# Ordering a three-block transformer kernel by a simulated timeline instead of the default heuristic

## The chip, the cores and the metric

The kernel runs on one core of a Trainium2 chip. A core has five engines with an instruction stream each: TensorE (PE in the profile, its weight loads PEld) multiplies matrices, VectorE (DVE), ScalarE (ACT) and GpSimd (POOL) work on tiles, and SyncE (SP) starts the DMA transfers. The engines meet only at semaphores. The metric is the device time of one execution in microseconds. Before the change it is 2908.86 us, the median of 3 runs from 2906.74 to 2912.71.

## The reference

The input is 512 tokens of 1024 numbers, which pass through three blocks in a row.

- The first block: RMS norm, one wide projection, sparse attention of 16 heads (compressed, selected and windowed keys, gated), a causal convolution of width 31 per channel with a layer norm behind it, an output projection, and a SwiGLU feed-forward layer.
- The second block: multi-scale pooling beside a gated delta net of 8 heads, an output projection with layer norm, an MLP with squared ReLU, and a gated side input. The delta net per head, cut to its core:

```
q, k, v = silu(conv4(x @ w))        # q and k normalised to length 1
m  = strictly_lower(beta * k @ k.T * decay)
u, w = solve(m + I, [v * beta, k * beta * exp(gc)])
for chunk n:                        # the recurrence
    v_new = u[n] - w[n] @ state
    o[n]  = qg[n] @ state + attn[n] @ v_new
    state = state * exp(gl[n]) + kg[n].T @ v_new
o = rms_norm(o) * o_norm_w * silu(z)
```

- The third block: stick-breaking attention (weights from a running sum of log-sigmoids along the keys) beside sliding-window attention, again with output projection, an MLP with squared ReLU, and a gated side input.

## The kernel before

All activations are kept transposed, as tiles of 128 features by 512 tokens. A gemm (`K.gemm`, L171 to L173) makes 128 output features: eight input tiles times three matmuls, since both weights and activations are split into a high and a low part (wh with the high part of the operand, wh with the low one, wl with the high one). Its result lies in a PSUM tile `pg`. A weight unit of 512 KB comes by DMA on SyncE into `wst` (2 buffers), ScalarE makes `wh` from it (L155), GpSimd `wl` (L156), with 4 buffers each. The gemms of the MLPs and projections make most of TensorE's work; the attention, the convolution and the delta net put small matmuls and much work of the other engines between them.

The delta net (`block2`) takes the heads one by one. `head_in` projects k, q and v of the next head (a gemm, a convolution of four taps L1308 to L1310, silu L1312 to L1313, normalisation L1321 to L1344). `chunks` builds the matrices of the head: transposes into KG and VB (L1371 to L1376), products of k with k and q (L1391) into MT and AT, the diagonal blocks written to memory and read back rearranged (dg, diag, B: DMA), their inverse Z by 30 small VectorE operations (L1416, L1417), Yi (L1420) and its transpose (L1425). Then come the levels 16, 32 and 64 of the inverse, each of which is a chain between TensorE and the others:

```
ps = MT.T @ Xi         # L1431   T1 = ps * level     # L1433 VectorE
ps = Yi.T @ T1         # L1437   Xi = Xi - ps        # L1439 VectorE
ps = transpose(Xi)     # L1443   Yi = copy(ps)       # L1445 ScalarE
last level: ps = T1.T @ Yi  # L1448   Yf = Yi - ps   # L1450 VectorE
```

`recur` runs the recurrence over four chunks of 128: k with the state S (L1462), t (L1464, VectorE), Yf with t (L1466), vn (L1468, ScalarE), the new state (L1471 on TensorE, S of L1474 or L1476 on VectorE), outputs into `po` (L1478, L1479), and then the output's copy, square, column sum (L1483, L1485, L1487) and norm (L1490). `merge` gates the output with two more gemms.

In the third block, `stick_scores` makes a head's scores (L1882 to L1884), takes them through exponent, logarithm, maximum, four scans and a last exponent into a weight tile z (L1887 to L1898), and `stick_mix` transposes z (L1907), splits it into PTh and PTl (L1779, L1780) and multiplies it with the values (L1909, L1910). `window_mix` (L1854 to L1858) does so for the windows.

In the first block VectorE has, beside the attention's operations, the 240 taps of the convolution (L673, on tiles `py`); ScalarE copies each finished channel tile (X, L674).

What sets the order: the kernel's text writes the work of the heads in an order given by strings of letters (`ORD`, `ORD2`, `ORD3`: which step of which generator comes next). The framework then orders the whole program anew. It plays the program on a model of the machine and takes, engine by engine, the ready instruction of the best priority; the priority goes by the text's position, shifted where the text says so: weight loads forward by `HP` (30, 60 and 0 places in the three blocks), the Z operations back by `SLO` = 50, the convolution's taps back by `LOW` = 3000. The order so made is fixed in the program; on the chip each engine runs its list from the front.

## Time and profile before

| what | value |
|---|---|
| median of 3 runs | 2908.86 us (2906.74 to 2912.71) |
| the profiled execution's own time | 2904.16 us |
| its span | 2902.4 us |
| mean granted TensorE clock | 0.972 |
| TensorE busy | 2676.3 us (92%) |
| VectorE busy | 1780.9 us (61%) |
| ScalarE busy | 1283.2 us (44%) |
| GpSimd busy | 1306.6 us (45%) |

Names of tiles stand in the profile without their numbers: `pg <- op,wh` is a matmul that reads the tiles op and wh and writes pg. L171 is line 171 of the kernel. "PE x <- DVE y" in a list of waits says that TensorE stood still ahead of the instruction that writes x until VectorE had written y. The granted clock is a share of the full clock. Idle time of an engine counts only where the chain that ends last passes over it.

### The profile page before, as it was taken

What the parts mean: (1) busy time and instruction counts of PE and PEld (TensorE: products, weight loads), DVE (VectorE), ACT (ScalarE), POOL (GpSimd) and SP (SyncE); (2) the same over time, 40 slices, a digit from 0 to 9 for tenths busy, and PEclk for the clock granted to TensorE, in tenths of its full rate; (3) what the DMA queues carried; (4) which work ended last, traced back from release to release, by engine and by line L of the source; (5) the groups of instructions that cost most, each with busy time, mean ns of one, the idle gap of its engine ahead of it and who ended that gap; (6) DMA issues with size and microseconds to landing.
All of it is one profiled execution on the core that took longest, in us unless ns stands there. A gap on an engine that the chain in (4) does not pass through costs nothing.

```text
span 2902.4 us, 34153 instructions
## 1 busy us (share of the span) xinstructions
PE 2676.3 (92%) x12206; PEld 2120.0 (73%) x12206; DVE 1780.9 (61%) x2825; ACT 1283.2 (44%) x2317; POOL 1306.6 (45%) x1023
## 2 busy tenths in 40 slices
PE   7899999699999988988889999999988889999997
PEld 5677776478888856766676788877766678788885
DVE  7889899965243596776774821126877765422246
ACT  4357875533222354444443533332556652322234
POOL 6554432554444454333332644454544344444443
PEclk9999999799999999999999999999999899999999
DMA  3321111232322222222222222232222122222223
GB/s 115 114 86 54 54 38 37 77 105 91 98 95 94 95 67 96 70 78 73 70 70 68 67 101 95 95 116 88 94 89 75 49 80 87 92 98 95 95 95 102
DMA packets 79193, 243.32 MB, mean 84 GB/s; under 512 B 11312, under 2 KB 15320, under 8 KB 79024
## 3 DMA queue, kind: packets, MB, share of 16 engines
q1 hardware_dynamic: 79024, 241.15, 25.3%
q8 instruction: 96, 1.57, 0.2%
q14 instruction: 73, 0.60, 0.1%
HBM read 230.96 MB, written 4.52 MB: 81 GB/s over the span
## 4 chain that ended last, share of the span: by engine, by line
PE 63%; DVE 23%; ACT 6%; DMA 3%; issue 3%; POOL 2%; SPq 0%; DVEq 0%; ACTq 0%; POOLq 0%
PE pg L172 18%; PE pg L173 18%; PE pg L171 18%; DMA B<-diag 2%; DVE p L1894 1%; DVE py L673 1%; DVE X L336 1%; DVE QK L1310 1%; PE ppt L956 1%; POOL wl L156 1%; DMA diag<-dg 1%; DVE ln L277 1%; DVE Zt L1416 1%; PE ps L934 1%; DVE Z L1417 1%
## 5 line engine op out<-in xcount | busy, mean ns | idle before, releaser
L156 POOL TENSOR_TENSOR wl<-wst,wh 128x512 fp32r<-128x512 f32 (+1 forms) x808 | 1099.9, 1367 | 1367.1 <-ACT wh L155 1285.7
L155 ACT ACTIVATE wh<-wst 128x512 fp32r<-128x512 f32 (+1 forms) x808 | 500.8, 627 | 1102.1 <-PE pg L172 918.1
L171 PE MATMUL pg<-op,wh 128*128 128x512 f32 (+1 forms) x2008 | 812.7, 405 | 38.9 <-ACT wh L155 19.5
L172 PE MATMUL pg<-op,wh 128*128 128x512 f32 (+1 forms) x2008 | 808.6, 403 | 2.6 <-DVE op L191 2.4
L173 PE MATMUL pg<-op,wl 128*128 128x512 f32 (+1 forms) x2008 | 807.2, 402 | 3.9 <-POOL wl L156 3.9
L171 PEld LDWEIGHTS pg<-op,wh 128*128 128x128 f32 (+1 forms) x2008 | 386.7, 193 | 120.9 <-ACT wh L155 20.1
L173 PEld LDWEIGHTS pg<-op,wl 128*128 128x128 f32 (+1 forms) x2008 | 386.2, 192 | 83.6 <-POOL wl L156 6.7
L172 PEld LDWEIGHTS pg<-op,wh 128*128 128x128 f32 (+1 forms) x2008 | 387.3, 193 | 82.2 <-DVE op L191 5.8
L171 PE MATMUL pg<-hid,wh 128*128 128x512 f32 x688 | 272.2, 396 | 0.9 <-DVE hid L190 0.9
L173 PE MATMUL pg<-hid,wl 128*128 128x512 f32 x688 | 272.1, 396 | 0.0
L172 PE MATMUL pg<-hid,wh 128*128 128x512 f32 x688 | 271.8, 395 | 0.2 <-DVE hid L191 0.2
L673 DVE SCALAR_TENSOR_TENSOR py<-z,vec,py 128x512 f32<-128x512 f32 x240 | 180.2, 751 | 10.9 <-ACT py L671 6.2
L1120 DVE TENSOR_TENSOR X<-X,pg 128x512 f32<-128x512 f32 x56 | 38.5, 688 | 222.1 <-PE pg L173 222.1
L171 PEld LDWEIGHTS pg<-hid,wh 128*128 128x128 f32 x688 | 129.2, 188 | 32.9 <-DVE hid L190 1.3
L172 PEld LDWEIGHTS pg<-hid,wh 128*128 128x128 f32 x688 | 129.2, 188 | 31.9 <-DVE hid L191 0.5
L173 PEld LDWEIGHTS pg<-hid,wl 128*128 128x128 f32 x688 | 129.2, 188 | 31.3 <-issue 0.2
L190 DVE CAST hid<-t 128x512 fp32r<-128x512 f32 x86 | 53.0, 616 | 145.7 <-ACT t L1097 145.0
L1111 DVE SCALAR_TENSOR_TENSOR t<-pg,R 128x512 f32<-128x512 f32 x32 | 22.1, 691 | 84.0 <-PE pg L173 83.9
L938 ACT ACTIVATE P<-ps,s 128x128 f32<-128x128 f32 (+3 forms) x128 | 66.4, 523 | 11.6 <-DVE s L937 9.5
L191 DVE TENSOR_TENSOR hid<-t,hid 128x512 fp32r<-128x512 f32 x86 | 63.6, 740 | 3.0
L937 DVE TENSOR_REDUCE s<-ps 128x1 f32<-128x128 f32 (+3 forms) x128 | 60.1, 483 | 8.1 <-PE ps L936 6.6
L960 DVE TENSOR_TENSOR PTl<-ppt,PTh 128x512 fp32r<-128x512 f32 x80 | 53.4, 684 | 4.7 <-ACT PTh L959 3.9
(523 smaller groups left out, 4344.3 us busy)
## 6 DMA issues: line engine op xcount, KB each, us to landing
wst<-in_w_f_dram SPq DMA_DIRECT2D x64, 512.0 KB
wst<-in_w_up_dram SPq DMA_DIRECT2D x32, 512.0 KB
wst<-in_w_down_dram SPq DMA_DIRECT2D x32, 512.0 KB
wst<-in_w_ga_dram SPq DMA_DIRECT2D x24, 512.0 KB
wst<-in_w_fg_dram SPq DMA_DIRECT2D x22, 512.0 KB
wst<-in_w_fu_dram SPq DMA_DIRECT2D x22, 512.0 KB
wst<-in_w_q_dram SPq DMA_DIRECT2D x16, 512.0 KB
wst<-in_w_out_dram SPq DMA_DIRECT2D x16, 512.0 KB
```

What stands on the lines that cost most here:

```text
L155: nc.scalar.activation(h, st, AF.Copy)
L156: nc.gpsimd.tensor_tensor(l, st, h, SUB)
L171: self.nc.tensor.matmul(ps, lhsT=wh, rhs=h[:, sl], start=first and k == 0, stop=False)
L172: self.nc.tensor.matmul(ps, lhsT=wh, rhs=l[:, sl], start=False, stop=False)
L173: self.nc.tensor.matmul(ps, lhsT=wl, rhs=h[:, sl], start=False, stop=last and k == n - 1)
L190: nc.vector.tensor_copy(h, src)
L191: nc.vector.tensor_tensor(l, src, h, SUB)
L673: nc.vector.scalar_tensor_tensor(y, z[:, k:k + T], w(k), y, op0=MUL, op1=ADD)
L937: nc.vector.tensor_reduce(mx[:, h:h + 1], S[:, :L], AX, MAX, negate=True)
L938: nc.scalar.activation(Pt[h][:, :L], S[:, :L], AF.Exp, bias=mx[:, h:h + 1], accum_out=den[:, h:h + 1])
L960: nc.vector.tensor_tensor(tl, pt, th, SUB)
L1120: nc.vector.tensor_tensor(X[:, m], X[:, m], ps, ADD)
```

## The change

One argument is added where the framework's context is opened. The framework then orders the whole program by a simulated timeline of all its engines instead of by its default heuristic. The text of the computation, the priorities and the number of buffers stay.

```
-    with tile.TileContext(nc) as tc:
+    with tile.TileContext(nc, schedule_with_timeline_sim=True) as tc:
         program(tc, I, out)
```

No matmul, activation, vector operation or DMA of the computation is added or removed. What differs is the order of each engine's list, and with it some semaphore instructions (on ScalarE 1048 for 997, on VectorE 254 for 225, on GpSimd 927 for 916) and table loads (74 for 77). The lists are the same, or nearly so, in the three MLPs; they differ in the first block's attention and convolution, in the delta net, and in the third block's attention.

The first place is TensorE in the middle of one delta-net head, at the second and third level of the inverse. `pg` rows are the gemm of another head's projection, `piv` are the inverse's tiles. Before:

```order
L1431 MATMUL piv_11054<-Xi_10975,MT_10781 128x128 x4
L172 MATMUL pg_11158<-op_9370,wh_11165 128x512
L173 MATMUL pg_11158<-op_9369,wl_11166 128x512
L171 MATMUL pg_11158<-op_9375,wh_11165 128x512
L172 MATMUL pg_11158<-op_9376,wh_11165 128x512
L1437 MATMUL piv_11061<-T_2380_11059,Yi_10982 128x128 x4
L173 MATMUL pg_11158<-op_9375,wl_11166 128x512
L171 MATMUL pg_11158<-op_9381,wh_11165 128x512
L172 MATMUL pg_11158<-op_9382,wh_11165 128x512
L173 MATMUL pg_11158<-op_9381,wl_11166 128x512
L1443 MATMUL piv_11068<-ident,Xi_11066 128x128 x4
```

and after the change, from the last gemm row ahead of the same steps:

```order
L173 MATMUL pg_11603<-op_9387,wl_11611 128x512
L1443 MATMUL piv_10977<-ident,Xi_10975 128x128 x4
L1431 MATMUL piv_11054<-Xi_10975,MT_10781 128x128 x4
L1437 MATMUL piv_11061<-T_2380_11059,Yi_10982 128x128 x4
L1443 MATMUL piv_11068<-ident,Xi_11066 128x128 x4
L1431 MATMUL piv_11143<-Xi_11066,MT_10781 128x128 x4
L1448 MATMUL piv_11150<-Yi_11073,T_2401_11148 128x128 x4
L1371 MATMUL piv_11204<-ident,QK_10811 128x128 x4
L1375 MATMUL piv_11210<-ident,vT_11008 128x128 x4
L1466 MATMUL prc_11247<-VB_10758,Yf_11155 128x128
L1391 MATMUL piv_11228<-QK_10811 128x256 x2
L1471 MATMUL prc_11251<-vn_11249,KG_10757 128x128
```

The gemm rows between the steps of the inverse are gone from there; they stand ahead of the first L1443 here, 41 gemm rows in a run with one step (L1437) among them. L1371, L1375 and L1391 belong to the next head, L1466 and L1471 are the first steps of this head's recurrence.

The second place is TensorE in the same head's recurrence, in its third chunk and after it. `prc` and `po` are the recurrence's tiles. Before:

```order
L1462 MATMUL prc_11429<-S_11321,QK_10366 128x128
L1478 MATMUL po_11246<-qg_10772,S_11321 128x128
L171 MATMUL pg_11454<-op_9327,wh_11457 128x512
L172 MATMUL pg_11454<-op_9328,wh_11457 128x512
L1466 MATMUL prc_11433<-t_2470_11431,Yf_11155 128x128
L173 MATMUL pg_11454<-op_9327,wl_11458 128x512
L171 MATMUL pg_11454<-op_9333,wh_11457 128x512
L1471 MATMUL prc_11437<-vn_11435,KG_10757 128x128
L1479 MATMUL po_11246<-AT_10782,vn_11435 128x128
L172 MATMUL pg_11454<-op_9334,wh_11457 128x512
L173 MATMUL pg_11454<-op_9333,wl_11458 128x512
L1462 MATMUL prc_11443<-S_11439,QK_10366 128x128
```

and after the change, from the third chunk's L1466 to the head's end:

```order
L1466 MATMUL prc_11433<-t_2470_11431,Yf_11155 128x128
L1471 MATMUL prc_11437<-vn_11435,KG_10757 128x128
L1479 MATMUL po_11246<-AT_10782,vn_11435 128x128
L1462 MATMUL prc_11443<-S_11439,QK_10366 128x128
L1478 MATMUL po_11246<-qg_10772,S_11439 128x128
L1466 MATMUL prc_11447<-t_2476_11445,Yf_11155 128x128
L1479 MATMUL po_11246<-AT_10782,vn_11449 128x128
L1487 MATMUL prc_11524<-os_11522,ones 128x512
L171 MATMUL pg_11815<-op_9327,wh_11818 128x512
```

Two gemm matmuls stood between L1462 and L1466, and between L1466 and L1471; now the third and fourth chunk follow each other without any, up to the output's column sum (L1487), behind which the next gemm starts.

The third place is TensorE at the end of the third block's attention, where the last head's weight tile z_19557 is transposed. `pg` rows are gemms of the output's gates. Before:

```order
L173 MATMUL pg_19770<-oo_17962,wl_19763 128x512
L171 MATMUL pg_19770<-oo_18279,wh_19762 128x512
L1907 MATMUL ppt_19633<-ident,z_19557 128x128 x4
L1907 MATMUL ppt_19644<-ident,z_19557 128x128 x3
L172 MATMUL pg_19770<-oo_18280,wh_19762 128x512
L173 MATMUL pg_19770<-oo_18279,wl_19763 128x512
L171 MATMUL pg_19770<-oo_18283,wh_19762 128x512
L1909 MATMUL po_19632<-PTh_19638,VA_19549 128x512
L172 MATMUL pg_19770<-oo_18284,wh_19762 128x512
L173 MATMUL pg_19770<-oo_18283,wl_19763 128x512
L1910 MATMUL po_19632<-PTl_19639,VA_19549 128x512
L1909 MATMUL po_19632<-PTh_19648,VA_19549 128x384
```

and after the change:

```order
L1910 MATMUL po_19590<-PTl_19607,VA_19549 128x384
L1907 MATMUL ppt_19621<-ident,z_19349 128x128
L1909 MATMUL po_19590<-PTh_19615,VA_19549 128x256
L1910 MATMUL po_19590<-PTl_19616,VA_19549 128x256
L1907 MATMUL ppt_19633<-ident,z_19557 128x128 x4
L1909 MATMUL po_19590<-PTh_19623,VA_19549 128x128
L1910 MATMUL po_19590<-PTl_19624,VA_19549 128x128
L1907 MATMUL ppt_19644<-ident,z_19557 128x128 x3
L1907 MATMUL ppt_19654<-ident,z_19557 128x128 x2
L1909 MATMUL po_19632<-PTh_19638,VA_19549 128x512
L1910 MATMUL po_19632<-PTl_19639,VA_19549 128x512
L1909 MATMUL po_19632<-PTh_19648,VA_19549 128x384
```

The gemm rows are gone from between the transposes (L1907) and the mix-in steps (L1909, L1910); ahead of these rows now stand the mix-in steps of the head before (po_19590), and no gemm since that head's scores.

## Rows read from the trace of the kernel before

**Rows 1.** The page: busy time by engine, and the chain that ended last.

```profile
PE 2676.3 (92%) x12206; PEld 2120.0 (73%) x12206; DVE 1780.9 (61%) x2825; ACT 1283.2 (44%) x2317; POOL 1306.6 (45%) x1023
...
PE 63%; DVE 23%; ACT 6%; DMA 3%; issue 3%; POOL 2%; SPq 0%; DVEq 0%; ACTq 0%; POOLq 0%
```

**Rows 2.** Stages: start:end, length, PE, PEld, DVE, ACT, POOL busy, PEclk, DMA share, GB/s.

```profile
500.00:550.00 50.00, 24.02 (x82) 16.89 (x81) 45.40 (x61) 19.40 (x28) 18.07 (x10) 0.69 0.06 21
...
1100.00:1600.00 500.00, 437.52 (x2126) 338.94 (x2126) 334.98 (x688) 225.86 (x368) 172.73 (x147) 0.96 0.24 75
...
1700.00:2050.00 350.00, 348.16 (x1510) 283.06 (x1509) 107.51 (x148) 116.29 (x196) 164.03 (x126) 1.00 0.29 98
2050.00:2400.00 350.00, 305.82 (x1391) 238.50 (x1390) 266.39 (x411) 201.53 (x358) 163.45 (x114) 0.94 0.24 77
```

**Rows 3.** TensorE's waits from 1150 to 1600: us in total, times, longest.

```profile
PE prc L1462 <- DVE S L1474: 18.2, 5, 5.3
PE prc L1466 <- DVE t L1464: 7.7, 5, 3.6
PE piv L1425 <- DVE Yi L1420: 7.0, 6, 2.3
PE piv L1391 <- DVE KG L1372: 5.1, 5, 1.2
```

**Rows 4.** The chain, 1350 to 1445: start, length, what.

```profile
1352.98 1.13 PE piv L1391 x4
...
1357.05 4.43 DMA diag<-dg
...
1361.54 7.05 DMA B<-diag
...
1376.35 0.23 PE pg L171
...
1377.98 0.60 ACT oT L1483
...
1384.85 0.30 DVE Yi L1420
...
1385.29 0.44 PE piv L1425 x2
...
1410.75 1.13 PE piv L1391 x4
...
1440.89 0.44 PE piv L1425 x2
```

**Rows 5.** VectorE's groups from 1150 to 1600: busy us, mean ns, idle before.

```profile
L1433 DVE TENSOR_TENSOR T<-piv,lev 128x512 f32<-128x512 f32 x24 | 16.5, 688 | 14.0 <-PE piv L1431 14.0
...
L1464 DVE SCALAR_TENSOR_TENSOR t<-prc,nbe,VB 128x128 f32<-128x128 f32 x24 | 8.3, 347 | 4.3 <-PE prc L1462 4.3
```

**Rows 6.** ScalarE's groups in the same stretch.

```profile
L1468 ACT ACTIVATE vn<-prc 128x128 f32<-128x128 f32 x32 | 8.8, 274 | 35.8 <-PE prc L1466 35.8
...
L1485 ACT ACTIVATE os<-oT 128x512 f32<-128x512 f32 x8 | 5.0, 629 | 0.0
```

**Rows 7.** Waits around 523, TensorE from 500 and ScalarE from 480 on.

```profile
PE pg L171 <- ACT wh L155: 18.7, 1, 18.7
...
ACT X L674 <- DVE py L673: 29.7, 2, 23.8
```

**Rows 8.** TensorE's waits from 2050 to 2400.

```profile
PE po L1910 <- DVE PTl L1780: 11.2, 6, 4.9
PE ppt L1854 <- DVE A L1842: 8.1, 10, 1.3
```

**Rows 9.** The chain, 2338 to 2366, a stick-breaking head's weights.

```profile
2344.37 0.07 PE ps L1884
...
2352.78 4.43 DVE p L1894 x4
...
2359.22 0.04 ACT z L1898
```

## Prediction

> **What bounds the kernel now.** I read the page first: TensorE works 2676.3 of 2902.4 us, and the chain that ended last lies on it for 63% and on VectorE for 23% [rows 1]. So the time is TensorE's work plus its idle time, about 226 us, and an order that removes and adds no computation can act on those 226 us alone (and on the clock). Next I cut the span into stages [rows 2]. In the MLP stretch from 1700 to 2050 TensorE is busy 348.16 of 350 us; order shows its rows there unchanged, and so for the other two MLPs. The idle time sits in three places: the first block from 0 to 550, with 26.0 us of it in its last 50 (50 less 24.02); the delta net from 1100 to 1600, with 62.5 us (500 less 437.52); and the third block's attention from 2050 to 2400, with 44.2 us (350 less 305.82). Then I asked each stage what TensorE waits for, and compared the two orders there.
>
> In the delta net TensorE waits mostly for VectorE: for the recurrence's state (L1462 for S of L1474, 18.2 us, and L1466 for t of L1464, 7.7), and at the inverse (L1425 for Yi, 7.0, L1391 for KG, 5.1) [rows 3]. One head follows another every 55.6 us, from the matmul of L1425 at 1385.29 to the same at 1440.89 [rows 4]. At 62.5 / 8 = 7.8 us of idle, a head holds 47.8 us of TensorE time.
>
> **What the change does, and its price.** No instruction of the computation is added or removed; some semaphore instructions come and go, and three table loads fewer stand on ScalarE, which is far from full. Nothing is lengthened. All that counts is which matmul stands in front of which, and how long VectorE's queue is when an operation comes up.
>
> *The delta net.* In the order before, gemm matmuls of the next projections (L171 to L173, 0.23 us each [rows 4]) stand between the small dependent steps of a head: between L1431 and L1437 four of them, then four more before L1443, about 0.9 us. That covers one VectorE step. So what TensorE waits there today isn't the steps' own length but VectorE being busy with something else (convolution and output operations). In the new order most of the gemms stand in one dense run, and the last inverse levels and most of the recurrence stand behind it with nothing between (the order's first two pieces). The dependent step is then bare. Its price is the operation plus 0.3 us for the last matmul to drain and two hand-overs, an estimate from the pieces of the chain: VectorE's Yi ends at 1385.15 and TensorE starts at 1385.29, and the last matmul's own 0.2 us is hidden by no successor. Counted from order for one head:
> - T (L1433) twice, 0.69 us [rows 5], and Xi (L1439) once, an operation of the same shape: 3 x 1.0 = 3.0;
> - vn (L1468) three times, 0.27 us [rows 6]: 3 x 0.57 = 1.7;
> - t (L1464) twice, 0.35 us [rows 5], and S (L1474), of the same shape, once, with one small matmul of 0.2 us between: 3 x 0.45 = 1.35;
> - the copy of the output (L1483, 0.60 [rows 4]) and its square (L1485, 0.63 [rows 6]) ahead of L1487: 1.5;
> - Yf, mostly behind eight transposes: 0.2.
>
> The sum is 7.75 us a head, 62 over eight. That equals the 62.5 us of today, but it is a floor of another kind: it comes from the order alone and holds with VectorE free, while today's comes from VectorE's queue. Whether queue time comes on top decides. The slowest loop says that it does. From L1391 of a head, over the diagonal's way through memory (4.43 and 7.05 us for two transfers) and the 30 small Z operations, to L1425 it takes 32.3 us now (1352.98 to 1385.29), and 30.1 in the next head (1410.75 to 1440.89) [rows 4]. Nothing in that path is shortened; order puts some more convolutions among the Z operations. In the new order TensorE has between these two points some 22 us of work (61 gemm matmuls, three recurrence steps, the output's sum; by the times that these very instructions took before, slow-clock ones included) plus 4.5 us of bare steps, so it waits at L1425. The rest of the head is 47.8 - 22 = 25.8 us of work and 3.2 of bare steps (T, Xi, T, Yf). A head then takes 30.1 to 32.3 plus 29.0, 59 to 61 us, against 55.6: 3.5 to 5.7 us a head, 28 to 46 in all. I take +30, near the lower end, since part of the 30 us is itself queueing that a calmer VectorE may return. Bounds: 0 (only the bare steps) to +60.
>
> The clock: TensorE's granted clock is 0.96 in the delta net and 0.69 in the 50 us before 550, where the engine stood idle for half of the time [rows 2]; the two levels are 1.2 and 2.4 GHz. A hundredth of mean clock over the delta net's 437.52 busy us is worth 437.52 / 96 = 4.6 us. I leave the clock as it is in the sum and put two hundredths, 9 us, into the range. The Trainium skill (TensorE: Matmul & The Clock Gate, Part 1) speaks against the change here: the default state of the clock is the throttled one and activity releases it, so that idle time gathered in one place costs its own length and then slow matmuls behind it. The rows of 500 to 550 agree; by that rule the sum would be some 9 us higher.
>
> *The third block.* Waits of the mix-in steps (L1910 for PTl 11.2, L1854 for A 8.1) make 19.3 us [rows 8]. In the new order these stand 15 to 35 us of TensorE work later, still between gemms, so I let three quarters go: -15. But the last stick-breaking heads are no longer mixed with gemms (the order's last two pieces). From the last score matmul (L1884 at 2344.37) to the transposes of its weights (L1907) there lies a chain of exponent, logarithm, four scans (4.43 us together) and more passes [rows 9]. Before, L1898 starts at 2359.22, some 15 us behind the matmul, and TensorE had gemms to do. Now eleven rows of small matmuls stand between (seven transposes and eight mix-in steps, some 2.4 us), so some 12 us show. Net -3, bounds -30 and +20 (waits all gone and the tail's chain overlapped by its neighbour, or waits kept and the tail bare).
>
> *The first block.* The convolution's 240 taps (L673) come earlier among VectorE's attention work. ScalarE's 29.7 us at X L674 behind the taps, and with it TensorE's 18.7 us for split weights, [rows 7] should go. But VectorE is the bound here, with 45.40 of those last 50 us busy [rows 2], and its total work up to the layer norm's feed is the same. The layer norm ends no earlier, so another wait takes the place: 0. Bounds: -18.7 if all of that wait is returned, and +20 if attention steps that are now behind taps, and whose last group has neither gates nor taps left to cover it, stretch VectorE's path.
>
> Sum: +30 - 3 + 0 = +27 on the profiled execution's 2904.16 us, 2931; that execution lies 4.7 us under the median of 2908.86, so on the runs 2936 us.
>
> **The rivals.**
> - *Faster: queues dissolve.* The new order places each operation where a simulation of all engines has it ready. VectorE's waits in the delta net and the third block are queue waits (18.2 us of S alone), which speaks for it; the bare steps, which no queue explains, speak against it. Delta net -10, third block -19, first block -15: some -44, 2865; with half of that 2887.
> - *Slower still: the loop L1391 to L1425 sets the pace everywhere.* If the bunched VectorE work (KG, VB, MT, AT, the state) makes this loop 33 to 34 us instead of 30 to 32, a head takes 62 to 63 us: +52 to +59, and the third block's tail +12 uncompensated: around 2970. It decides from 33 us between L1391 and L1425 on. For it: VectorE's work in a head is 334.98 / 500 x 55.6 = 37 us, and it now stands in fewer places.
> - *Nothing.* VectorE's queue returns in the delta net what the bare steps cost, and elsewhere gains and losses cancel: 2909. The count of 62 against 62.5 us speaks for it. The change does reorder (the order's rows show that), so no effect at all is not in question.
>
> **Chances.** Forecast 0.52, faster 0.22, slower still 0.16, nothing 0.10. Two runs differ by up to 0.2%, some 6 us, which is the least that can be told from no change. The forecast's own range is 2912 to 2960; a tenth of it falls within 6 us of before. So slower 0.52 x 0.9 + 0.16 + a little of nothing = 0.65, no change 0.12, faster 0.23. To leave no more than 2 in 10 out, the range reaches from 2885 (half of the faster case) to 2980.
>
> **What would show it.** In the changed kernel's windows the delta net should be 25 to 45 us longer at the same busy time. Its waits should name L1437 and L1448 for T, L1443 for Xi, L1471 for vn and L1487 for os, about 1 us each time and eight times, none of which is among the great ones now; L1425 for Yi should grow from 7.0 towards 20 to 30. L1425 of two heads should lie 59 to 61 us apart. The wait of L171 for wh at 523 should be gone, with the layer norm (L198) in its place and the first block ending within 20 us of before. In the third block L1910 and L1854 should shrink, and L1907 for z grow to 10 or more. I am wrong if the heads keep 55 to 56 us, if the delta net's idle time falls, or if the first block ends much earlier or later.

## The result, and the profile after

The changed kernel takes 3003.89 us (median of 4 runs, 3000.98 to 3014.65) against 2910.78 (2906.74 to 2914.30) for the kernel before in the same comparison: a ratio of 1.0329 [1.031, 1.0347], slower by 93 us by the medians and 96 by the ratio. Forecast were 27 us, in a range that ended at 2980. The profiled execution spans 3003.8 us against 2902.4, and these 101.4 us are what the rows can split; some 8 of them are the scatter of single executions.

The page, as in [rows 1]: the same 12206 matmuls are busy 56.6 us longer.

```profile
PE 2732.9 (91%) x12206; PEld 2174.0 (72%) x12206; DVE 1762.4 (59%) x2825; ACT 1282.8 (43%) x2314; POOL 1302.2 (43%) x1023
```

To place the loss I took the start of every TensorE instruction in both traces and subtracted. The new kernel is 9 us behind where the delta net begins, 102 where it ends, 108 in the second MLP and 101 in the third. So the first block cost 9, the delta net 93, the stretch right behind it 6, and the third block gave back 7. The delta net, from the first matmul of L1371 to the last of L1487, is one row in each kernel (start:end, length, busy of PE, PEld, DVE, ACT, POOL, PEclk, DMA share, GB/s), here that of before:

```profile
1139.40:1572.40 433.00, 376.65 (x1887) 292.55 (x1886) 297.67 (x641) 193.06 (x314) 146.76 (x124) 0.96 0.24 73
```

and here that of after, with the end of the first block, which answers to [rows 2]:

```profile
500.00:550.00 50.00, 45.34 (x197) 32.03 (x197) 39.23 (x62) 32.80 (x67) 15.87 (x10) 0.93 0.06 22
...
1148.70:1674.60 525.90, 423.73 (x1891) 330.35 (x1892) 288.50 (x640) 195.49 (x315) 144.22 (x125) 0.85 0.20 61
```

Of the delta net's 92.9 us, 45.8 are idle time (525.90 - 423.73 = 102.2 against 433.00 - 376.65 = 56.4) and 47.1 are busy time of the same work. Most of the longer busy time goes with a lower clock: PEclk is 0.85 instead of 0.96. By the trace's records of the granted clock TensorE stood at 1.2 GHz for 34.1 us of the stretch before and 154.1 after, and was busy for 31.5 and 116.2 of these. Half of the second difference, 42 us, is put down to the slow level; what is left of the 47.1, some 5 us, is not explained. In the table below "clock cost" is always half of the busy time at 1.2 GHz. That half is an estimate, from the distance of two gemm matmuls in the new delta net: 0.23 us ahead of 1405 and 0.43 from 1421.80 on. It says how long TensorE worked slowly, and not yet that the time would come back at full clock; the runs with useless matmuls ask that.

What TensorE waits for in the new delta net, to be held against [rows 3]:

```profile
PE prc L1466 <- DVE t L1464: 28.0, 20, 3.1
PE prc L1487 <- ACT os L1485: 10.8, 8, 1.3
...
PE piv L1448 <- DVE T L1433: 7.0, 8, 0.9
PE piv L1443 <- DVE Xi L1439: 6.8, 9, 0.8
PE piv L1437 <- DVE T L1433: 6.8, 8, 0.9
PE prc L1471 <- ACT vn L1468: 6.7, 17, 0.4
...
PE po L1479 <- ACT vn L1468: 3.4, 8, 0.4
PE piv L1425 <- DVE Yi L1420: 3.3, 3, 1.5
PE piv L1375 <- DVE Yf L1450: 2.9, 7, 0.4
```

The rows with T and Xi, eight or nine waits of 0.9 us at most, are the bare steps: the same wait, once in each head. The first row is another thing: t comes 20 times and up to 3.1 us late. One head's inverse and recurrence show them in TensorE's timeline (start, length, instruction; in brackets the idle time ahead of it and what ended it):

```profile
1405.38 0.60 PE L1443 MATMUL piv<-ident,Xi 128*128 128x128 f32 x4
1405.81 1.06 PE L1431 MATMUL piv<-Xi,MT 128*128 128x128 f32 x8
1407.74 1.13 PE L1437 MATMUL piv<-T,Yi 128*128 128x128 f32 x8 [0.88 <-DVE T L1433]
1409.65 0.66 PE L1443 MATMUL piv<-ident,Xi 128*128 128x128 f32 x4 [0.78 <-DVE Xi L1439]
1410.15 1.06 PE L1431 MATMUL piv<-Xi,MT 128*128 128x128 f32 x8
1412.08 1.13 PE L1448 MATMUL piv<-Yi,T 128*128 128x128 f32 x8 [0.88 <-DVE T L1433]
...
1420.00 0.49 PE L1466 MATMUL prc<-t,Yf 128*128 128x128 f32 x2 [1.78 <-DVE t L1464]
1420.86 0.49 PE L1471 MATMUL prc<-vn,KG 128*128 128x128 f32 x2 [0.37 <-ACT vn L1468]
1421.18 0.39 PE L1479 MATMUL po<-AT,vn 128*128 128x128 f32 x2
1421.35 0.66 PE L171 MATMUL pg<-op,wh 128*128 128x512 f32 x1
```

No gemm matmul stands between. The windows of the same head show what follows (length, PE busy, PEclk, DMA share, GB/s):

```profile
1395.00:1405.00 10.00, 10.00 (x53) 1.00 0.33 107
1405.00:1421.00 16.00, 10.51 (x72) 1.00 0.18 57
1421.00:1431.00 10.00, 8.17 (x32) 0.83 0.31 71
1431.00:1441.00 10.00, 6.47 (x16) 0.54 0.26 79
```

The bare stretch itself still runs at full clock with 5.5 of 16 us idle. The slow level comes behind it, and the first gemm of L171 there is shown with 0.66 us, where those ahead of 1405 have 0.39. So the fall is paid by what follows between the next head's L1391 and L1425, its 51 to 61 gemms and the recurrence: there TensorE is busy at 1.2 GHz for 11 to 14.5 us in each of the six middle heads. In the dense run behind L1425 the records show the full clock again.

The heads (from one head's L1371 to the next) took 55.6, 51.9, 55.8, 57.8, 55.6 and 54.9 us before, and take 63.5, 65.1, 64.4, 64.8, 63.7 and 62.8 now, the first head left out of both. In three pieces: L1371 to L1425 31 to 37, now 39; L1425 to L1448 15, now 24; L1448 to the next L1371 5.5, now 1. The six heads between add up to 52.7 of the 92.9 us, and the other 40 lie at the two ends. From the first head's L1371 to the second's it takes 71.3 us instead of 45.4, but 87 more matmul rows (281 against 194) run there. The last head takes 70.3 instead of 56.0 with 41 rows fewer (221 against 262), at a granted clock of 0.71 instead of 0.97. One head in two pieces, L1391 to L1425 and from there to the next L1391 (columns as above), before:

```profile
1351.30:1385.30 34.00, 26.85 (x112) 20.30 (x112) 21.49 (x58) 12.29 (x21) 9.78 (x10) 0.90 0.34 102
1385.30:1409.10 23.80, 21.40 (x126) 17.15 (x126) 18.64 (x28) 13.06 (x20) 8.70 (x7) 1.00 0.07 23
```

and after:

```profile
1350.30:1388.20 37.90, 29.51 (x107) 21.74 (x107) 26.33 (x67) 14.49 (x25) 8.64 (x9) 0.77 0.18 51
1388.20:1414.80 26.60, 23.06 (x133) 19.20 (x132) 10.81 (x18) 11.22 (x16) 9.38 (x7) 1.00 0.23 78
```

In the third block the waits of the mix-in steps fell as forecast, against [rows 8]. The wait for z is the first line here, before and after; it was 8.0 us already:

```profile
PE ppt L1907 <- ACT z L1898: 8.0, 4, 2.8
```

```profile
PE ppt L1907 <- ACT z L1898: 13.4, 4, 9.1
...
PE po L1910 <- DVE PTl L1780: 2.9, 6, 0.9
...
PE ppt L1854 <- DVE A L1842: 2.2, 3, 0.9
```

### The profile page after: what moved, and what is told of

Same layout as the page of the kernel before. It is cut to its first block, busy times and chain, and to the rows that moved or that the text cites. A ratio compares the mean times of both kernels' runs of the same rounds, so it can differ in the third digit from the quotient of the medians.

```text
span 3003.8 us, 34245 instructions
## 1 busy us (share of the span) xinstructions
PE 2732.9 (91%) x12206; PEld 2174.0 (72%) x12206; DVE 1762.4 (59%) x2825; ACT 1282.8 (43%) x2314; POOL 1302.2 (43%) x1023
## 3 DMA queue, kind: packets, MB, share of 16 engines
q1 hardware_dynamic: 79024, 241.15, 24.4%
## 5 line engine op out<-in xcount | busy, mean ns | idle before, releaser
L171 PE MATMUL pg<-op,wh 128*128 128x512 f32 (+1 forms) x2008 | 802.6, 401 | 38.8 <-DVE zb L653 11.2
L172 PE MATMUL pg<-op,wh 128*128 128x512 f32 (+1 forms) x2008 | 799.2, 398 | 8.2 <-DVE op L191 7.9
L173 PE MATMUL pg<-op,wl 128*128 128x512 f32 (+1 forms) x2008 | 798.1, 398 | 2.8 <-POOL wl L156 2.8
L171 PEld LDWEIGHTS pg<-op,wh 128*128 128x128 f32 (+1 forms) x2008 | 385.6, 192 | 136.2 <-issue 15.6
L172 PEld LDWEIGHTS pg<-op,wh 128*128 128x128 f32 (+1 forms) x2008 | 385.5, 192 | 90.8 <-DVE op L191 11.2
L171 PE MATMUL pg<-hid,wh 128*128 128x512 f32 x688 | 271.4, 395 | 0.0
L172 PEld LDWEIGHTS pg<-hid,wh 128*128 128x128 f32 x688 | 129.2, 188 | 31.5 <-issue 0.2
L171 PEld LDWEIGHTS pg<-hid,wh 128*128 128x128 f32 x688 | 129.2, 188 | 31.3 <-issue 0.2
L934 PE MATMUL ps<-sk,sk 128*128 128x256 f32 (+2 forms) x128 | 52.3, 409 | 19.5 <-ACT P L938 16.2
```

Source lines behind the costliest of these rows:

```text
L171: self.nc.tensor.matmul(ps, lhsT=wh, rhs=h[:, sl], start=first and k == 0, stop=False)
L172: self.nc.tensor.matmul(ps, lhsT=wh, rhs=l[:, sl], start=False, stop=False)
L173: self.nc.tensor.matmul(ps, lhsT=wl, rhs=h[:, sl], start=False, stop=last and k == n - 1)
L934: nc.tensor.matmul(S[:, :N], lhsT=ql, rhs=kh[:, :N], start=True, stop=False)
```

## The experiments

The two kernels differ in thousands of places of TensorE's list alone, so nearly all experiments hold the order of one or more engines by a list, within the delta net, and leave the rest to the kernel's own scheduler. The lists name the instructions that ran from 1105 to 1605 us in the kernel before (1769 on TensorE). A dependency between neighbours of a list, on the same engine and without a semaphore, gives the order of that engine. An engine without a list is ordered anew by the scheduler around the lists, so its order in the delta net can be neither that of before nor that of after. How far it went is told below as the rows outside the longest sequence that two traces have in common, by operation and tiles; the two kernels themselves differ by 221 of 640 rows on VectorE, 129 of 313 on ScalarE and 26 of 123 on GpSimd. The lists go in like this:

```diff
+def pin(tc, *orders):
+    at = {i.name: i for i in tc.nc.cur_bb.bb.instructions}
+    info = mybir.DependencyInfo(mybir.DependencyClass.NoSync, mybir.DependencyReason.DATA)
+    for text in orders:
...
+        for p, n in zip(names, names[1:]):
+            tc.add_manual_dep(at[n], p, info, reason="pin")
...
         program(tc, I, out)
+        pin(tc, PE_ORDER)
```

"After" as a base has the timeline simulation on, "before" has it off. Medians and ratios are against the kernel before on the same chip, and the columns behind them are the profile's, for the delta net.

| run | base, and the edit | median | ratio | length | idle | clock cost |
|---|---|---|---|---|---|---|
| (before) | | 2910.78 | | 433.0 | 56.4 | 15.8 |
| (after) | | 3003.89 | 1.0329 [1.031, 1.0347] | 525.9 | 102.2 | 58.1 |
| a_dn_before | after; order of PE, DVE, ACT, POOL of before | 2922.55 | 1.0034 [1.0023, 1.0046] | 436.7 | 60.1 | 16.0 |
| a_pe_before | after; PE of before | 2963.77 | 1.0188 [1.0171, 1.0206] | 479.4 | 89.2 | 31.6 |
| a_pe_dve_before | after; PE and DVE of before | 2940.58 | 1.0096 [1.0081, 1.0111] | 450.9 | 68.8 | 20.3 |
| a_pe_act_before | after; PE and ACT of before | 2945.19 | 1.0106 [1.0091, 1.0121] | 466.9 | 79.8 | 31.2 |
| b_pe_after | before; PE of after | 3009.05 | 1.0345 [1.0326, 1.0364] | 535.4 | 115.8 | 56.8 |
| b_bare_levels | before; inverse's last levels bare | 2952.52 | 1.0136 [1.0119, 1.0153] | 476.8 | 86.9 | 31.1 |
| b_bare_fill | the same, useless matmuls in between | 2936.89 | 1.0097 [1.0081, 1.0114] | 461.9 | 63.2 | 17.9 |
| a_fill | after; useless matmuls in bare steps | 3010.62 | 1.0344 [1.0324, 1.0363] | 521.4 | 87.0 | 43.0 |
| a_t_early | after; DVE: t ahead of Z | 3005.03 | 1.0328 [1.0306, 1.035] | 525.5 | 112.1 | 46.9 |
| a_ts_early | after; DVE: t and S ahead of Z | 3009.80 | 1.0348 [1.0332, 1.0364] | 528.4 | 113.0 | 48.6 |
| a_rec_early | after; DVE: t, S and t ahead of Z | 3005.89 | 1.0329 [1.0307, 1.035] | 529.2 | 104.2 | 62.8 |
| a_k_late | after; DVE: k's convolution behind Yi | 3043.16 | 1.0461 [1.0438, 1.0483] | 561.1 | 127.4 | 68.1 |
| a_t_k | after; both of these moves | 3040.87 | 1.0450 [1.0435, 1.0465] | 554.6 | 127.0 | 63.4 |
| a_levels_early | after; PE: gemms between the steps again | 2981.36 | 1.0239 [1.0221, 1.0257] | 491.4 | 93.1 | 36.3 |
| b_s_early | before; DVE: S, mt, q's and k's convolution and t ahead of Z | 2899.74 | 0.9967 [0.9955, 0.998] | 423.2 | 50.6 | 11.2 |
| b_s_early2 | the same, v's convolution later | 2905.48 | 0.9988 [0.9978, 0.9997] | 429.7 | 57.0 | 10.8 |

**Whose order costs.** The first pair gives TensorE's order of one kernel to the other.

```diff
+        pin(tc, PE_ORDER)   # a_pe_before: base after, TensorE's list of before
+        pin(tc, PE_ORDER)   # b_pe_after: base before, TensorE's list of after
```

> The changed kernel (timeline order everywhere), but TensorE's matmuls of the delta net (1769 of them, those that ran from 1105 to 1605 us before) are held in the order that they had before the change; VectorE, ScalarE, GpSimd and the DMAs stay as the timeline simulation orders them. Theory A, the loss is TensorE's order in the delta net, its gemms no longer standing between the dependent steps: the delta net's 93 us come back, 3004 falls to 2905-2920, the granted clock of the stretch returns to 0.95 or more. Theory B, the loss comes from the order of VectorE and ScalarE: little comes back, 2970-3004. If both count: 2930-2960.

> The kernel before, with only TensorE's matmuls of the delta net held in the order of the changed kernel; the other engines stay with the default order. Theory A (TensorE's order alone): 2911 + 85 to 100 = 2995-3010, clock of the delta net down to about 0.85. Theory B (the other engines' order): 2911-2940.

Holding TensorE's new list alone makes the old kernel as slow as the new one. Putting the old list back in the new kernel returns only 40 of the 93 us. In lengths of the delta net: 433 before, 535 with TensorE's new list held, 479 with its old list held, 526 after. This is not TensorE's order by itself, as the expectation took it. In b_pe_after the other engines did not keep the order of before: 222 rows of VectorE's and 131 of ScalarE's differ from it, as many as in the new kernel, and only 165 and 36 differ from the new kernel's. In a_pe_before they differ from before by 129 and 55, from the new kernel by 214 and 131. So a list for TensorE draws the other orders after it, under either scheduler, and no run held TensorE's new list beside the other three old ones. What TensorE's order costs by itself is not shown. The row of b_pe_after, and the wait that leads there:

```profile
1139.60:1675.00 535.40, 419.60 (x1891) 329.97 (x1892) 280.32 (x640) 197.10 (x315) 143.20 (x125) 0.84 0.19 60
```

```profile
PE pg L171 <- ACT cz L1306: 33.4, 11, 3.7
PE prc L1466 <- DVE t L1464: 11.3, 20, 0.9
PE prc L1487 <- ACT os L1485: 10.8, 8, 1.3
PE prc L1462 <- DVE S L1474: 10.3, 7, 1.7
PE piv L1448 <- DVE T L1433: 7.0, 8, 0.9
```

The dense gemm run now stops for ScalarE's eviction of a convolution's input (cz, L1306), a wait that is 0.5 us in the new kernel, whose other engines are ordered otherwise. T, Xi and os wait as in the new kernel.

What else of the others' order counts was asked with three more lists:

```diff
-        pin(tc, PE_ORDER)
+        pin(tc, PE_ORDER, DVE_ORDER, ACT_ORDER, POOL_ORDER)   # a_dn_before
+        pin(tc, PE_ORDER, DVE_ORDER)                          # a_pe_dve_before
+        pin(tc, PE_ORDER, ACT_ORDER)                          # a_pe_act_before
```

> The changed kernel with TensorE, VectorE, ScalarE and GpSimd all held in the delta net (instructions that ran from 1105 to 1605 us before) in the order before the change; only the DMAs' order there, and all else in the program, are the timeline's. With TensorE's order alone held, the delta net still took 479 us (433 before, 526 changed). Theory A2, the rest lies in the order of the other engines' lists: 2905-2920, delta net 430-440 us. Rival: it lies in the DMAs' order (weights, diagonal blocks) or is carried in from the first block: 2940-2965.

> The same with TensorE and VectorE held as before, ScalarE and GpSimd the timeline's. If VectorE's order (convolution operations ahead of the recurrence's t and S) makes the remaining 46 us: delta net 433-445, 2905-2925. If ScalarE's order makes them (its copies cz, mt and sh late): 2945-2965.

> The same with TensorE and ScalarE held as before, VectorE and GpSimd the timeline's. If VectorE's order makes the remaining 46 us: 2950-2965. If ScalarE's: 2905-2925. If each makes a part: both this run and the one with VectorE held between 2920 and 2950.

With all four lists the delta net is back at 436.7 us and the time at +10: the loss lies in the order of these four engines in the delta net. Of the 10 us that stay, 8 lie ahead of it (its first matmul comes at 1147.6 instead of 1139.4). Beside this run the other two have one difference each. In a_pe_act_before VectorE is left to the timeline (112 rows differ from before, 1 on ScalarE and 3 on GpSimd): 22.6 us. In a_pe_dve_before ScalarE and GpSimd are (44 and 11 rows): 18.0 us. The two make 40.7 us, and a_pe_before, with all three left to it, is 41.2 slower than a_dn_before (some 45 by the ratios, since it ran on another chip).

The third block's gain was tried the other way round:

```diff
+        pin(tc, PE_ORDER, DVE_ORDER, ACT_ORDER, POOL_ORDER)   # before; the lists of after, 2040 to 2410 us
```

> The kernel before, with TensorE, VectorE, ScalarE and GpSimd held in the order of the changed kernel in the third block's attention alone (instructions that ran from 2040 to 2410 us before). By the two traces the changed order gains 6 to 7 us between the second block's end and the last MLP (shift 107.7 us before it, 100.8 behind it): 2902-2906. Rival: that gain is only the weights and operands that a late delta net let the other engines prepare, so none of it shows here: 2909-2915.

2906.68 us, 0.9993 [0.9984, 1.0001]: no difference that can be told. The 7 us that the new kernel gains in its third block do not come with the order of the four engines there alone.

**What a bare step costs.** In b_bare_levels TensorE's gemms between the last two levels of the inverse are moved ahead of these, 103 matmuls over the eight heads. Nothing else is edited, but the scheduler moved 100 of VectorE's 640 rows and 22 of ScalarE's 313 with it.

```diff
+L171 MATMUL pg_10367<-op_9339,wh_10370 128x512
+L1431 MATMUL piv_10003<-Xi_9994,MT_9917 128x128 x4
+L1437 MATMUL piv_10010<-T_2131_10008,Yi_10001 128x128 x4
+L1443 MATMUL piv_10017<-ident,Xi_10015 128x128 x4
+L1431 MATMUL piv_10252<-Xi_10015,MT_9917 128x128 x4
 L1448 MATMUL piv_10259<-Yi_10022,T_2183_10257 128x128 x4
```

> The kernel before, with TensorE's order of the delta net held as it was but for 103 gemm matmuls (13 a head) that stood between the inverse's second and third level steps (from the second L1431 to L1448): they are moved just ahead of these steps, so that T, Xi and T of each head are bare. The default order elsewhere. Price of the prediction, 3.0 us a head: 2909 + 20 to 28 = 2929-2937, with idle time up by as much. Theory C (idle time in one place lowers the clock too): 2940-2960, with the 1.2 GHz time of the delta net doubled from 34 us. Rival, the steps lie in slack because VectorE sets the pace of the delta net: 2905-2920.

Idle time grows by 30.5 us, where three steps of 1.0 us in eight heads make 24, and busy time by 13.3 (clock cost by the half: 15.3): 43.8 in all, 5.5 us a head for what the prediction priced at 3.0. A part of it can be the moved rows: the wait of L1462 for S is 26.8 us, 18.2 in [rows 3]. Whether the clock's part is a cost of its own, or only fills time that would be idle otherwise, b_bare_fill tells. It keeps the bare order and sets 96 matmuls that nothing needs into the three steps, into a bank that the step's own matmul overwrites. The other engines' orders are those of b_bare_levels but for a row on each of two, so this pair differs by the fill alone.

```diff
+    def fill(ps, L, R):
+        for c in cc:
+            nc.tensor.matmul(ps[:, c], lhsT=L[:, c], rhs=R[:, c], start=True, stop=True)
...
+                if k > 2:
+                    fill(ps, MT, Xi)
...
+                fill(ps, MT, Xi)
```

> The kernel before with the inverse's second and third level bare (103 gemm matmuls moved ahead of them; alone that made 2952, idle time of the delta net +30 us, time at 1.2 GHz 34 to 82 us), and now four useless matmuls of 128x128, overwritten at once, ahead of the steps L1437, L1443 and L1448 of these levels: 96 groups of work that stand in the waits, 0.8 us a group at the full clock against about 1 us of wait. Theory C (the clock's fall costs time of its own): the time at 1.2 GHz falls back below 55 us and the kernel to 2928-2944 although work is added. Theory D (the clock costs nothing of its own): 2948-2960.

The rows of the two, b_bare_levels first:

```profile
1142.20:1619.00 476.80, 389.94 (x1888) 308.97 (x1886) 298.84 (x640) 193.15 (x314) 144.45 (x124) 0.91 0.22 66
```

```profile
1142.10:1604.00 461.90, 398.65 (x2080) 319.95 (x2079) 298.96 (x640) 192.10 (x313) 142.95 (x124) 0.94 0.22 68
```

The fill adds 22 us of work at full clock (398.65 - 17.9 against 389.94 - 31.1) and takes 23.6 of idle away, which would leave the time as it was. The delta net is 14.9 us shorter and the median 15.6 lower; the two runs were on different chips, and by their ratios to the kernel before it is 11 us. That is near the clock cost's 13.2 alone: the lower clock costs time of its own here, and it can be had back by work that computes nothing.

In a_fill the same was done in the new kernel, with a fourth place ahead of L1487 (128 matmuls).

```diff
+        fill(ps, AT, qg)
```

> The changed kernel with TensorE's order of the delta net held, and in it four matmuls of 128x128 of no use (overwritten at once by the real ones) ahead of each of four bare steps of a head: two levels' L1437 and L1448, L1443 between them, and L1487; 128 matmuls in all, 0.19 us each at the full clock, which stand where TensorE waits anyway about 1 us. Theory C, half of the loss is the clock, which falls because TensorE stands idle in one place (154 us at the 1.2 GHz level against 34 before): the slow time falls by a third or more and the time falls to 2975-2995 though work is added. Rival D, the clock only goes with the idle time and costs nothing of its own (the slow matmuls lie in waits), or the added work does nothing for it: 3004-3020.

The waits on T, Xi and os are gone, idle falls by 15 and the clock cost by 15, for 26 us of work added. The delta net is 4.5 us shorter, the median not lower: L171 now waits 18.1 us for cz and L1466 still 29.9 for t. So the heads stay at 64 us without the bare steps and with 15 us less of clock cost. This run isn't the new kernel with a fill alone, though: 83 of VectorE's 639 rows and 31 of ScalarE's 314 moved, and on ScalarE an operation of the output's norm (L1488 in the kernel) with two table loads now stands ahead of cz, whose wait was 0.5 us.

**What holds the heads.** Two theories were left: the recurrence (t and S stand behind the Z operations in VectorE's list, and these wait for a transfer), and the loop from L1391 over that transfer, Z and Yi to L1425. VectorE's timeline in the new kernel shows both:

```profile
1365.79 0.77 DVE L1416 TENSOR_TENSOR Zt<-B,Z 128x60 f32<-128x60 f32 x1 [6.01 <-DMA B<-diag]
...
1366.98 0.34 DVE L1464 SCALAR_TENSOR_TENSOR t<-prc,nbe,VB 128x128 f32<-128x128 f32 x1
...
1371.83 1.40 DVE L1310 SCALAR_TENSOR_TENSOR QK<-cz,vec,QK 128x512 f32<-128x512 f32 x2
1373.15 0.18 DVE L1416 TENSOR_TENSOR Zt<-B,Z 128x32 f32<-128x32 f32 x1
1373.25 1.41 DVE L1310 SCALAR_TENSOR_TENSOR QK<-cz,vec,QK 128x512 f32<-128x512 f32 x2
...
1381.07 0.70 DVE L1313 SCALAR_TENSOR_TENSOR vT<-t,vT 128x512 f32<-128x512 f32 x1 [3.09 <-ACT t L1312]
...
1387.49 0.90 DVE L1420 TENSOR_TENSOR Yi<-Z,lev 128x128 f32<-128x128 f32 x4
```

VectorE stands idle for 6 us in front of Zt with t behind it; and from Zt to Yi it takes 21.7 us, 16.2 in the head at the same place before (1368.62 to 1384.85), with the convolutions of q and k in pairs and 3.1 us for a ScalarE result in between. Two moves in VectorE's list, tried apart and together:

```diff
+L1464 SCALAR_TENSOR_TENSOR t_2252_10541<-prc_10539,nbe,VB_9894 128x128
 L1416 TENSOR_TENSOR Zt_10437<-B_10354,Z_10435 128x4x15
...
-L1308 TENSOR_SCALAR QK_10366<-cz_10674,vec 128x4x128
...
 L1420 TENSOR_TENSOR Yi_10468<-Z_10435,lev 128x128 x4
+L1308 TENSOR_SCALAR QK_10366<-cz_10674,vec 128x4x128
+L1310 SCALAR_TENSOR_TENSOR QK_10366<-cz_10674,vec,QK_10366 128x4x128 x3
```

The first piece is a_t_early, the second a_k_late, both a_t_k.

> The changed kernel, TensorE and VectorE held in the delta net in its own order, with one move in VectorE's list: the recurrence's t (L1464, third chunk) of six heads, which stands behind the first Z operation (L1416) and with it waits for the transfer of B although its inputs are ready about 3.5 us earlier, goes ahead of that operation. Theory P, TensorE's own list (bare steps, slow clock) sets the head's 64.4 us: TensorE gets on 3.5 us earlier in six heads, 2980-2990. Theory L, the loop from L1391 over the diagonal's transfers and the Z operations to L1425, 37.5 us in the changed kernel against 30 to 32 before, sets it: 2998-3006.

> The changed kernel, held in the same way, with another move in VectorE's list: of the two convolutions that stand between the Z operations of six heads, that of k (L1308, three L1310 and L1313, some 3.4 us) goes behind the last Yi (L1420), so that the Z operations end earlier. Theory L (that loop sets the head): L1391 to L1425 shorter by about 3.4 us, heads 61 us, 2980-2990. Theory P (TensorE's list): 2998-3010.

> Both moves together. Theory P: as with the first alone, 2980-2990. Theory L: as with the second alone, 2980-2990. If both lie in one closed loop (t holds up TensorE ahead of L1425, the Z operations hold up L1425 itself) neither alone gives much and both together 2965-2985.

No gain, and a loss of some 39 us with k's convolution moved: L1323 waits 24.4 us for sh, and heads take 70 us. From Zt to Yi it takes 19 to 20.6 us in five of the six middle heads instead of 20.9 to 21.9, and still L1425 comes no earlier behind L1391 (37 to 39 us). With t moved alone, its wait passes to S:

```profile
PE prc L1462 <- DVE S L1474: 20.6, 7, 6.1
PE prc L1466 <- DVE t L1464: 14.3, 14, 1.8
```

So S and then the second t were moved as well.

```diff
+L1464 SCALAR_TENSOR_TENSOR t_2252_10541<-prc_10539,nbe,VB_9894 128x128
+L1474 SCALAR_TENSOR_TENSOR S_10549<-S_10431,eGL,prc_10547 128x128
+L1464 SCALAR_TENSOR_TENSOR t_2258_10555<-prc_10553,nbe,VB_9894 128x128
 L1416 TENSOR_TENSOR Zt_10437<-B_10354,Z_10435 128x4x15
```

> The changed kernel, TensorE and VectorE held in the delta net in its own order, but in six heads both the recurrence's t (L1464) and the next S (L1474) go ahead of the first Z operation, which waits for the transfer of B. With t alone ahead, S took the wait (L1462 for S: 1.6 us before the move, 20.6 behind it). Theory P (TensorE's list, the recurrence held up behind the transfer in VectorE's list): waits of L1466 and L1462 down by 20 us together, 2975-2990. Theory L (another loop of the head, over k's projection, convolution and the scores, closes on TensorE's list): 2998-3008, with the wait in a new place.

> The changed kernel, TensorE and VectorE held in the delta net in its own order, with all that is left of the recurrence in VectorE's list (t, S and the last t, L1464 and L1474) ahead of the first Z operation in six heads. With t alone ahead, S took the wait; with t and S ahead, the last t took it (L1466 34.2 us), since 13 Z operations and a convolution stood ahead of it. Theory P (the recurrence behind VectorE's list paces the heads): the wait of L1466 falls by 20 us or more and the kernel to 2975-2992. Theory L (another loop closes on TensorE's list, L1391 over the transfers and Z to L1425 above all): the waits fall but L1425's grows, 2998-3010.

In a_ts_early the wait passes to the last t (34.2 us). In a_rec_early the wait for t is down to 12.8 and the heads are as long as ever (five of 64.5 to 64.8 us, one of 61.4); the time is spent in front of a gemm:

```profile
PE pg L171 <- ACT cz L1306: 22.3, 6, 4.4
PE prc L1466 <- DVE t L1464: 12.8, 14, 1.8
```

So the recurrence's place behind the transfer does not set the pace by itself. But ScalarE's order is another here too: in five heads the two operations of the output's norm (L1488, L1489), each with a table load, moved ahead of cz, which can be why TensorE now waits for cz.

The same trace answers for the loop over the transfer. The last row of Yi is written 3.0 to 4.0 us ahead of L1425 in all six middle heads, with 14 to 16 us from Zt to Yi, as short as before, and the loop L1391 to L1425 still takes 36.4 to 37.9 us. One of them, Yi's operation and L1425:

```profile
1388.46 0.88 DVE L1420 TENSOR_TENSOR Yi<-Z,lev 128x128 f32<-128x128 f32 x4
```

```profile
1392.40 0.60 PE L1425 MATMUL piv<-ident,Yi 128*128 128x128 f32 x4
```

In b_pe_after Yi is done 9 to 14 us ahead of L1425 and heads take 66 to 68. In these runs TensorE's own list comes last. In the new kernel the two come to L1425 within half a microsecond of each other in five of six heads, with TensorE busy right up to it. The last run went at TensorE's list: four gemm rows ahead of each step of the inverse, as in the kernel before, the others between the steps of the recurrence.

```diff
+L1431 MATMUL piv_9982<-Xi_9975,MT_9917 128x128 x4
 L172 MATMUL pg_10564<-op_9340,wh_10567 128x512
 L173 MATMUL pg_10564<-op_9339,wl_10568 128x512
 L171 MATMUL pg_10564<-op_9345,wh_10567 128x512
 L172 MATMUL pg_10564<-op_9346,wh_10567 128x512
+L1437 MATMUL piv_9989<-T_2125_9987,Yi_9970 128x128 x4
```

> The changed kernel with TensorE held in the delta net in its own order but for one thing: of the dense run of 41 to 60 gemm matmuls between L1425 and L1448 of a head, four now stand ahead of each step of the inverse's levels, and what is left goes behind L1448, two ahead of each step of the recurrence, the rest after its second chunk. Nothing else is held. Measured before this run: from L1371 to L1425 39 us (35 before the change), from L1425 to L1448 24 us (15), from L1448 to the next L1371 1 us (5.5). Theory S (the gemm work in the levels lies in series with the loop over the transfers of diag and B, and is no longer beside it): L1425 to L1448 falls to 14-16 us, a head from 64.4 to 55-58, the kernel to 2940-2965, and the time at 1.2 GHz in the delta net from 154 to below 80 us. Rival, the projections that go behind L1448 are wanted by the next head's L1371: heads 61 us and more, 2980-3010.

L1425 to L1448 shrank from 24 to 13.4 us as expected, and heads from 64.4 to 61, not to 55 to 58: L1371 to L1425 grew from 39 to 46.5, and L1466 waits longer for t.

```profile
PE prc L1466 <- DVE t L1464: 38.0, 14, 5.7
```

Of the 93 us 22.5 came back; the rest was given back in the other piece of the head, where 84 to 104 gemms run now instead of 51 to 61. Yi is ready 15 us and more ahead of L1425 there, so that piece is set by TensorE's own list, its waits included. VectorE's order moved too (151 of 639 rows), so what the gemms between the steps are worth alone isn't shown.

**A version that beats both.** The same view of the kernel before shows S, an output step (L1509) and the convolution of q and k behind a Zt that waits 6.6 us for its transfer. In b_s_early they and the next t stand ahead of it in five heads, and in two more t alone; the lists of the other engines are held as they were.

```diff
 L1464 SCALAR_TENSOR_TENSOR t_2361_10986<-prc_10984,nbe,VB_10313 128x128
 L1509 SCALAR_TENSOR_TENSOR mt_10960<-mt_10960,pg_10925 128x512
+L1474 SCALAR_TENSOR_TENSOR S_10994<-S_10876,eGL,prc_10992 128x128
+L1308 TENSOR_SCALAR QK_10811<-cz_10847,vec 128x4x128
+L1310 SCALAR_TENSOR_TENSOR QK_10811<-cz_10847,vec,QK_10811 128x4x128
+L1464 SCALAR_TENSOR_TENSOR t_2367_11000<-prc_10998,nbe,VB_10313 128x128
+L1310 SCALAR_TENSOR_TENSOR QK_10811<-cz_10847,vec,QK_10811 128x4x128 x2
 L1416 TENSOR_TENSOR Zt_10882<-B_10799,Z_10880 128x4x15
```

> The kernel before with its own order held on TensorE, VectorE, ScalarE and GpSimd in the delta net, and one kind of move in VectorE's list: what stands behind the first Z operation (L1416), and so waits with it for the transfer of B, but is needed or ready earlier (S of L1474, mt of L1509, the convolution of QK, t of L1464) goes ahead of it, in five heads, and t alone in two. S was ready 3.8 and 5.6 us before VectorE took it up in the two heads that I looked at; TensorE's wait for it (L1462, 18.2 us) should go, and the Z operations run with less between them, so that L1425's 7.0 us shrink: 2885-2897. If the convolution's wait for the recurrence then stands in the Z operations' way instead: 2905-2920.

2899.74 us, 0.9967 [0.9955, 0.998]: 9 us faster than the kernel before and 104 faster than the changed one. S was the greatest wait of [rows 3] with 18.2 us; it fell to 3.3, and another took its place at the top. The move is one package; which of its rows gave the gain was not tried apart.

```profile
PE pm L1323 <- ACT sh L1321: 14.4, 6, 4.8
...
PE prc L1462 <- DVE S L1474: 3.3, 1, 3.3
```

b_s_early2 went at that one: L1323 and L1324 later on TensorE, v's convolution behind Yi on VectorE.

```diff
 L1420 TENSOR_TENSOR Yi_10913<-Z_10880,lev 128x128 x4
+L1308 TENSOR_SCALAR vT_11008<-cz_11044,vec 128x512
+L1310 SCALAR_TENSOR_TENSOR vT_11008<-cz_11044,vec,vT_11008 128x512 x3
```

> The kernel before with the move that made it 9 us faster (S, mt, the convolution of QK and t ahead of the first Z operation), and three more in five heads: the column sums L1323 and L1324 of q, which TensorE now waits for (14.4 us), go seven rows behind L1487; vT's convolution goes behind the last Yi instead of between the Z operations (some 2.7 us in the way of L1425); its tanh on ScalarE goes behind the copy L1426. 2900 less 5 to 15 us: 2883-2895. If vT's later convolution then holds up the next head's L1375: 2897-2910.

It is not better than b_s_early.

## Why the prediction was wrong, point by point

- *The direction and the place were right, and most bare steps.* T, T and Xi came to 20.6 us (counted: 24), vn to 10.1 (13.6), os to 10.8 (12), Yf to 3.8 with its two places (1.6), each with the longest wait under a microsecond or little over. But t and S, counted as 10.8, came to 32.0, of which t is 28.0 in 20 waits: in one chunk it stands behind the convolution's taps (1.8 us) and in the next behind a Zt that waits for the transfer (2.2 to 3.1), and it was priced as bare.
- *The step that failed is the stretch from L1391 to L1425.* The prediction gave TensorE there "some 22 us of work" plus "4.5 us of bare steps, so it waits at L1425", on a loop taken at 30.1 to 32.3 us since "Nothing in that path is shortened". Counted in the same way, from the second row of L1391 (1416.09 to 1452.3), one head's loop takes 36.2 us in the new kernel; from the first row, 36.9 to 39.9, where before it took 28.8 to 34.0. TensorE is busy there for 26.3 to 29.8 us and idle for 7 to 9 in five of the six heads (13.5 in the sixth), and it does not wait at L1425: that wait for Yi was to grow from 7.0 towards 20 to 30 us and is 3.3. The work was right at full clock (20.5 to 23.0 us), but by the half it costs 5.5 to 7.2 more. VectorE's Z stretch grew too, from 16.2 to 21.7 us in one head, with the convolutions in pairs and the wait for ScalarE's tanh. The rest of a head was taken at 29.0 us and takes 23.0 to 27.3. So L1425 of two heads lie 64.1 us apart (1388.24 and 1452.3) and not 59 to 61. The rival *Slower still* had the loop and the point from which it decides (33 us), and gave heads of 62 to 63 us.
- *The clock was mis-sized.* "I leave the clock as it is in the sum and put two hundredths, 9 us, into the range." It fell by eleven hundredths, which by the prediction's own price of 4.6 us are 51, and by the records 42. This could be seen: the bare steps gather idle time in one place, and the prediction had the row of 500 to 550 in which a stretch with half its time idle shows 0.69. The rule of the Trainium skill that stood against the change (TensorE: Matmul & The Clock Gate, Part 1) had the sign, and the trace agrees (0.85 instead of 0.96); the cost put beside it was too small. That the fall is a cost is shown for the kernel before with three bare steps (b_bare_fill against b_bare_levels). In the new kernel it is not: a_t_early, a_ts_early and a_fill have 9 to 15 us less of clock cost and are no faster, for TensorE waits longer or works more instead.
- *Eight equal heads.* The price was multiplied by eight. The six heads between lost 52.7 us, where 3.5 to 5.7 each make 21 to 34; the first and the last lost 40 together, a part of it work that runs in another head now.
- *The first block:* 0 forecast, +9. The wait at 523 is gone as said (TensorE is busy 45.34 of 500 to 550, 24.02 before), and idle time up to the delta net falls from 96.7 to 89.7 us. The layer norm did not take its place (L198 waits 1.9 us for ln, 6.7 before). Instead waits show up in the attention: idle time up to 450 us grows from 44.1 to 55.7, and up to 560 us L934 waits 16.2 us for ScalarE's P, where it waited 1.3. TensorE's busy time at 1.2 GHz grows up to the delta net from 47.4 to 65.3, by the half 9 us, and 25 more matmuls of the projections run ahead of it, some 6 us at 0.23. None of this was tried by itself.
- *The third block:* -3 forecast, -7. The mix-in waits fell by 14.2 (19.3 to 5.1; forecast -15). L1907's wait for z grew to 13.4, but only by 5.4: the +12 of the forecast left out the 8.0 us that stood there already. So the sum came near with one term more than twice too large. b_block3_after shows that the order of the four engines in this block alone does not give the 7 us.

What stays open: why the heads keep 64 us. It is shown that the four engines' orders in the delta net make the loss (a_dn_before). Neither the recurrence behind the transfer nor the loop over the transfer sets the pace by itself: with the first moved ahead and Yi 3 to 4 us early the heads stay (a_rec_early). Each of these runs took one wait away, and the stretch L1391 to L1425 came out at 36 to 40 us with another in its place, partly since unheld engines were ordered anew. Why the simulated timeline prefers the bunched order was not tried.

## What to carry to other kernels

Put independent matmuls between dependent steps, a few ahead of each, and don't let an order gather them in one run: three bare steps a head cost 30.5 us of idle time, and 13 of longer busy time on top (b_bare_levels). When forecasting an order, price the clock from a row of the same kernel where TensorE stands idle as much as it will. Look in an in-order list for short operations behind one that waits for a transfer: moving these was worth 9 us in the kernel before and nothing in the changed one. An order made by a simulation of all engines lost 93 us here. When holding one engine's order, look what the scheduler did to the others: here it moved up to two fifths of an engine's rows in the delta net (b_pe_after).

## What the runs showed of the hardware that was not expected

- Work that nothing needs made a kernel faster: 96 matmuls in the bare steps, 22 us of work, took 11 to 16 us off (b_bare_fill against b_bare_levels; granted clock 0.91 to 0.94 in the delta net). In the changed kernel 128 of them gave nothing (a_fill).
- The clock's fall shows behind the bare stretch and not in it: granted 1.00 from 1405 to 1421 with a third of the time idle, then 0.83 and 0.54 over the work that follows.
- A wait taken away often moved instead of going: t to S (28.0 to 14.3, with 20.6 new), S back to t (34.2), t to cz (22.3, with ScalarE's order moved as well), at the same time within the intervals.
